# Ten of eleven gated sections with the weights loaded into TensorE and the tokens streamed, in a one-core decoder layer

## The chip, the core and the metric

The kernel runs on one NeuronCore of a Trainium2 chip. The metric is the device time of one execution in microseconds; the median of three runs is compared.

## The reference, cut to what matters

One decoder layer on 256 tokens of 2048 features: an attention mixer, a layer norm, a gated feed-forward unit with 5632 inner features, a second layer norm. The change lies in the gated unit:

```
def swiglu(x, w_gate, w_up, w_down):
    return (jax.nn.silu(x @ w_gate) * (x @ w_up)) @ w_down

x = layer_norm(ALPHA * x + h, ln1_g[i], ln1_b[i])
x = layer_norm(ALPHA * x + swiglu(x, ffn_w_gate[i], ffn_w_up[i], ffn_w_down[i]), ln2_g[i], ln2_b[i])
```

All data are float32. `x` is 256 x 2048, `w_gate` and `w_up` are 2048 x 5632, `w_down` is 5632 x 2048.

## The kernel before

Every product is made from three matmuls on parts that TensorE takes in one pass: an operand is split into a rounded part `hi` and a remainder `lo` (`split`, L67: ScalarE writes `hi`, VectorE writes `lo`), and hi·hi, hi·lo and lo·hi are accumulated in PSUM. Each matmul instruction comes with a weight load (LDWEIGHTS, shown as engine PEld) of its 128x128 stationary operand.

The weights pass through once as a stream of sections: four for query, key and value (`q`), two for the output projection (`o`), eleven for gate and up (`f0` to `f10`, `FU`), one for the down projection (`d`). A section `f_i` takes 512 columns of gate and 512 of up, over 2048 contraction rows: eight pairs of 128-row slices. The SyncE queue loads a piece (a pair, 512 columns), ScalarE and VectorE split it, and TensorE uses it. The order is written out by hand: `blocks` is a list of blocks of matmuls, each for one pair and one half `m` of the tokens (128 of them), alternating between the halves; pieces are loaded and split `AHEAD` = 3 blocks before their first use, and other work is hung behind numbered blocks with `after` and `before`. Engines work through their instructions in that order.

In `block` (L215) the 128 tokens of a half are the stationary operand (`lh`, `ll`) and 512 weight columns stream past them: per slice and half two matmuls of L227 and L228 for each of gate and up, then one of L231 for each. So the sums `acc` have tokens on partitions and gate or up columns along the free side; four banks of PSUM serve a section (two halves, gate and up). There are eight banks.

The down projection wants the gated values the other way round, with inner features on partitions. So `gate_evac` (L412) takes silu of the gate bank on ScalarE and multiplies it with the up bank on VectorE into `hn`, and two blocks later `gate_t` (L420) turns `hn` by four TensorE transposes of 128x128 into a bank `ht`, which ScalarE copies to `hT`. `split_h` splits it before the down projection uses it. The layer norm's output is turned the same way in `ln1_t` (L370) into `x1T`, features on partitions: one pair of tiles for each half `m` and 1024 features.

Other places that the text below speaks of: `at_o` (L298) is the last product of a head of attention; it has six matmuls at L309, three that stream 256 columns and three that stream 128, each with a load of its own. The down projection's blocks run through the same `block` as before; a pair there has 48 matmuls.

Of the kernel before, what the change touches and what calls it, by code (L numbers as in the profile page):

```python
# [10 lines left out]
F = mybir.dt.float32  # L11
R = mybir.dt.float32r
AF = mybir.ActivationFunctionType
OP = mybir.AluOpType

P = 128
S = 256
# [8 lines left out]
CW = 512  # L26
# [15 lines left out]
def decoder_layer(ctx: ExitStack, tc: tile.TileContext, x, xt, rel_bias, w_qkv, w_o, g1, b1, gb1,  # L42
                  w_gate, w_up, w_down, g2, b2, c_ident, c_hot, c_mask, out):
    nc = tc.nc
# [7 lines left out]
    def p4(shape, dt, name):  # L52
        return sb.tile(shape, dt, tag="p4", bufs=P4, name=name)

    def s2(shape, dt, name):
        return sb.tile(shape, dt, tag="s2", bufs=S2, name=name)
# [4 lines left out]
    def bank(name):  # L61
        return ps.tile([P, CW], F, tag="b", bufs=8, name=name)

    def f32(t):
        return t.bitcast(F)

    def split(hi, lo, src):  # L67
        nc.scalar.activation(hi, src, AF.Copy)  # L68
        nc.vector.tensor_tensor(lo, src, f32(hi), op=OP.subtract)  # L69
# [59 lines left out]
        hi, lo = xT[kt // 4]  # L129
        return hi[:, kt % 4, m * P:(m + 1) * P], lo[:, kt % 4, m * P:(m + 1) * P]  # L130

    # ---- sections of the weight stream
    oT = {}

    def o_lhs(kt, m):
# [3 lines left out]
    x1T = {}  # L139

    def x1_lhs(kt, m):
        hi, lo = x1T[m, kt // 8]
        return hi[:, kt % 8, :], lo[:, kt % 8, :]

    hS = {}

# [5 lines left out]
    WO = [Sec(f"o{i}", [(w_o, 2 * i + c) for c in range(2)], 8, o_lhs) for i in range(2)]  # L152
    NF = FF // CW
    FU = [Sec(f"f{i}", [(w_gate, i), (w_up, i)], 8, x1_lhs) for i in range(NF)]
    DN = Sec("d", [(w_down, c) for c in range(4)], FF // (2 * P), h_lhs)

    blocks, ticks = [], {}

    def add(sec, pairs, m, chunks=None, ks=(0, 1)):
        blocks.append((sec, pairs, m, range(len(sec.chunks)) if chunks is None else chunks, ks))  # L160
        return len(blocks) - 1

    def alternate(sec, a, b):
        for p in range(a, b):
            add(sec, [p], 0)
            add(sec, [p], 1)
# [8 lines left out]
    k = 8 - SKEW_WO  # L175
# [2 lines left out]
    f0_t = [[add(FU[0], [p], m) for p in range(SKEW_F)] for m in range(2)]  # L178
    alternate(FU[0], SKEW_F, 8)
    for s in FU[1:]:  # L180
        alternate(s, 0, 8)
    k = DN.npair - SKEW_D
    alternate(DN, 0, k)
    dn_p = list(range(k, DN.npair))
# [2 lines left out]
    first, last = {}, {}  # L187
# [4 lines left out]
    start = {k: t - AHEAD for k, t in first.items()}  # L192
# [13 lines left out]
    def split_piece(s, p, c):  # L206
# [5 lines left out]
        split(hi, lo, r)  # L212
        s.pieces[p, c] = (hi, lo)

    def block(s, pairs, m, chunks, ks):  # L215
        for c in chunks:
            if (m, c) not in s.acc:
                s.acc[m, c] = bank(f"acc_{s.name}_{m}_{c}")
        nk = 2 * s.npair
        for p in pairs:  # L220
            for k in ks:
                kt = 2 * p + k
                lh, ll = s.lhs(kt, m)
                for c in chunks:
                    hi, lo = s.pieces[p, c]
                    a = s.acc[m, c]
                    nc.tensor.matmul(a, lh, hi[:, k, :], start=kt == 0, stop=False)  # L227
                    nc.tensor.matmul(a, lh, lo[:, k, :], start=False, stop=False)  # L228
                for c in chunks:
                    hi, lo = s.pieces[p, c]  # L230
                    nc.tensor.matmul(s.acc[m, c], ll, hi[:, k, :], start=False, stop=kt == nk - 1)  # L231

    # ---- attention
    SC = HD ** -0.5
    grp = {}

# [85 lines left out]
            steps += one  # L322
        return steps

    # ---- layer norms
    y_t, ln = {}, {}

    def load_ln(gam, bet, name):
# [16 lines left out]
    def ych(m, c):  # L345
        return y_t[m, c // 2][:, (c % 2) * CW:(c % 2 + 1) * CW]
# [21 lines left out]
        nc.vector.tensor_scalar(y, y, ln["mv", m][:, 0:1], ln["r", m], op0=OP.subtract, op1=OP.mult)  # L368

    def ln1_t(m, c):  # L370
        if c % 2 == 0:
            x1T[m, c // 2] = (p4([P, 8, P], R, "x1h"), p4([P, 8, P], R, "x1l"))
        src = ych(m, c)
        b = bank("tr")
        t = s2([P, CW], F, "x1f")
        for j in range(4):
            js = slice(j * P, (j + 1) * P)
            nc.tensor.transpose(out=b[:, js], in_=src[:, js], identity=ident)
        for j in range(4):
            js = slice(j * P, (j + 1) * P)  # L380
            k = 4 * c + j
            g, s = gbT[:, k:k + 1], gbT[:, 16 + k:17 + k]
            if j < 3:
                nc.scalar.activation(t[:, js], b[:, js], AF.Identity, scale=g, bias=s)
            else:
                nc.vector.tensor_scalar(t[:, js], b[:, js], g, s, op0=OP.mult, op1=OP.add)
        hi, lo = x1T[m, c // 2]
        a = 4 * (c % 2)
        split(hi[:, a:a + 4, :], lo[:, a:a + 4, :], t.rearrange("p (j c) -> p j c", j=4))

    def ln1_affine(m, c):
        y = ych(m, c)
# [13 lines left out]
            eng.tensor_tensor(y, y, pch(1, c), op=OP.add)  # L406
        nc.sync.dma_start(out[m * P:(m + 1) * P, c * CW:(c + 1) * CW], y)

    # ---- gated unit
    hn, hT = {}, {}  # L410

    def gate_evac(i, m):  # L412
# [7 lines left out]
    def gate_t(i, m):  # L420
# [5 lines left out]
            nc.tensor.transpose(out=b[:, j * P:(j + 1) * P], in_=t[:, j * P:(j + 1) * P], identity=ident)  # L426
        nc.scalar.activation(hT[i][:, :, m * P:(m + 1) * P], b.rearrange("p (j c) -> p j c", j=4), AF.Copy)

    def split_h(i):
        t = hT.pop(i)  # L430
        hi, lo = p4([P, 4, S], R, f"hh{i}"), p4([P, 4, S], R, f"hl{i}")
        split(hi, lo, t)
        hS[i] = (hi, lo)

    # ---- what goes between the blocks
    pre, post = {}, {}

    def before(t, f, *a):
# [2 lines left out]
    def after(t, f, *a):  # L441
        post.setdefault(t, []).append((f, a))
# [25 lines left out]
    for m, at in ((0, [wo_t[1][0], wo_t[1][0], wo_t[1][1], f0_t[0][0]]),  # L468
                  (1, [f0_t[0][2], f0_t[0][2], f0_t[0][3], f0_t[1][0]])):
        for c in range(4):  # L470
            after(at[c], ln1_t, m, c)
    after(first["f1", 0], load_ln, g1, b1, "ln1")
    for m in range(2):
        for c in range(4):
            after(first["f1", 0] + 8 + 2 * (4 * m + c), ln1_affine, m, c)
    for i in range(NF):
        for m in range(2):
            t = last[f"f{i}", m]
            after(t, gate_evac, i, m)
            after(min(t + 2, first["d", 0]), gate_t, i, m)  # L480
    after(dn_t[0][0] - 12, load_ln, g2, b2, "ln2")
    for i in range(NF):
        t = first["d", 2 * i]
        before(t - 3 if i else t - 1, split_h, i)
# [13 lines left out]
    s = Q[0]  # L498
# [8 lines left out]
    for k in range(2):  # L507
        split_x(0, slice(k, k + 1))
        for c in range(3):
            hi, lo = s.pieces[0, c]  # L510
            split(hi[:, k, :], lo[:, k, :], s.raws[0, c][0][:, k, :])
    n = 0
    for t, blk in enumerate(blocks):
        for f, a in pre.get(t, []):
            f(*a)
        while n < len(order) and order[n][0] <= t:
            _, _, ss, p = order[n]
            if ss is Q[0]:
                load_x(p, slice(0, 2))
                split_x(p, slice(0, 2))  # L520
            for c in range(len(ss.chunks)):
                split_piece(ss, p, c)
            n += 1
        block(*blk)
        for f, a in post.get(t, []):
            f(*a)
# [49 lines left out]
```

## Time and profile before

| | us |
|---|---|
| median of three runs | 1147.78 (1147.64 to 1148.76) |
| span of the profiled execution, first to last instruction | 1145.1 |
| TensorE busy in it | 1125.9 (98%) |
| VectorE busy | 612.3 (53%) |
| ScalarE busy | 492.2 (43%) |

The profiled execution's own time beyond its span is not given apart; its span lies 2.7 us under the median. TensorE's two rows, PE and PEld, overlap: a weight load runs while an earlier matmul streams. Matmuls overlap as well, so the mean duration of one matmul is longer than the distance from its start to the next one's start. The distance of starts (called the pitch below) is what adds up to time.

### The profile page before, as it was taken

Reading aid. Unit: us, or ns where it says so; the run is one execution under the profiler, and the core shown is the slowest. Engines: PE = TensorE matmul, PEld = TensorE weight load, DVE = VectorE, ACT = ScalarE, POOL = GpSimd, SP = SyncE. Lnnn points to the kernel's source line nnn. Section 1 sums busy time; section 2 is a strip of 40 time slices with the busy share of each in tenths; the row PEclk is TensorE's granted clock in tenths of the full one; section 3 lists DMA queues with packets and bytes.
Section 4 is the critical chain, followed back from the end, with each engine's and each line's share of the span. In section 5 each row is a group of like instructions: output and inputs, shape, how many; then the busy total and the mean of one; then the engine's idle time right before and its main releaser. Section 6 shows DMA issues by size and latency. Waiting matters only on the chain.

```text
span 1145.1 us, 13392 instructions
## 1 busy us (share of the span) xinstructions
PE 1125.9 (98%) x5139; PEld 929.8 (81%) x5139; DVE 612.3 (53%) x737; ACT 492.2 (43%) x623; POOL 12.6 (1%) x20
## 2 busy tenths in 40 slices
PE   9989999999999999999999999999999999999995
PEld 6868888888888888888888888888888888888884
DVE  6535556664568664582452543542544555454456
ACT  6434444444455474362452442542533544344320
POOL 0000000000000000000000000000000000000002
PEclk9999999999999999999999999999999999999998
DMA  9996555554466627663653744745647565548611
GB/s 336 233 249 234 177 172 165 184 177 158 158 224 215 245 82 266 224 196 138 254 186 139 264 144 153 256 144 185 225 142 258 174 222 199 196 147 309 205 56 74
DMA packets 62816, 222.29 MB, mean 194 GB/s; under 512 B 7104, under 2 KB 7536, under 8 KB 62752
## 3 DMA queue, kind: packets, MB, share of 16 engines
q1 hardware_dynamic: 61472, 216.19, 54.3%
q0 software_dynamic: 1280, 5.24, 3.0%
q8 instruction: 40, 0.66, 0.2%
q14 instruction: 24, 0.20, 0.1%
HBM read 216.16 MB, written 5.24 MB: 193 GB/s over the span
## 4 chain that ended last, share of the span: by engine, by line
PE 93%; DMA 3%; issue 2%; DVE 1%; POOL 0%; ACT 0%; SPq 0%; DVEq 0%; POOLq 0%; ACTq 0%
PE acc_f L227 14%; PE acc_f L228 14%; PE acc_f L231 14%; PE acc_q L227 7%; PE acc_q L231 7%; PE acc_q L228 7%; PE acc_d L228 6%; PE acc_d L231 6%; PE acc_d L227 6%; DMA r_q<-in_w_qkv 3%; PE acc_o L227 3%; PE acc_o L228 3%; PE acc_o L231 3%; PE ov L309 1%; PE lg L266 1%
## 5 line engine op out<-in xcount | busy, mean ns | idle before, releaser
L227 PE MATMUL acc_f<-wh_f,x1h 128*128 128x512 f32 x704 | 276.4, 393 | 0.0
L228 PE MATMUL acc_f<-wl_f,x1h 128*128 128x512 f32 x704 | 274.2, 389 | 0.0
L69 DVE TENSOR_TENSOR wl_f<-r_f,wh_f 128x1024 fp32r<-128x1024 f32 x176 | 207.7, 1222 | 100.5 <-ACT wh_f L68 72.7
L231 PE MATMUL acc_f<-wh_f,x1l 128*128 128x512 f32 x704 | 216.9, 389 | 0.0
L68 ACT ACTIVATE wh_f<-r_f 128x1024 fp32r<-128x1024 f32 x176 | 177.2, 1054 | 78.9 <-PE acc_f L228 56.0
L69 DVE TENSOR_TENSOR wl_d<-r_d,wh_d 128x1024 fp32r<-128x1024 f32 x88 | 103.2, 1221 | 96.7 <-ACT wh_d L68 65.9
L231 PEld LDWEIGHTS acc_f<-wh_f,x1l 128*128 128x128 f32 x704 | 132.2, 188 | 27.8
L227 PEld LDWEIGHTS acc_f<-wh_f,x1h 128*128 128x128 f32 x704 | 132.2, 188 | 26.8
L228 PEld LDWEIGHTS acc_f<-wl_f,x1h 128*128 128x128 f32 x704 | 132.3, 188 | 26.7
L227 PE MATMUL acc_q<-wh_q,xh 128*128 128x512 f32 x372 | 149.2, 401 | 3.8 <-ACT qn L243 3.8
L228 PE MATMUL acc_q<-wl_q,xh 128*128 128x512 f32 x372 | 146.1, 393 | 1.0 <-DVE wl_q L69 1.0
L227 PE MATMUL acc_d<-wh_d,hh 128*128 128x512 f32 x352 | 137.0, 389 | 0.0
L228 PE MATMUL acc_d<-wl_d,hh 128*128 128x512 f32 x352 | 136.9, 389 | 0.0
L69 DVE TENSOR_TENSOR wl_q<-r_q,wh_q 128x1024 fp32r<-128x1024 f32 x93 | 109.5, 1222 | 50.2 <-ACT wh_q L68 49.6
L68 ACT ACTIVATE wh_d<-r_d 128x1024 fp32r<-128x1024 f32 x88 | 87.0, 1050 | 100.9 <-PE acc_d L228 79.7
L68 ACT ACTIVATE wh_q<-r_q 128x1024 fp32r<-128x1024 f32 x93 | 93.4, 1054 | 39.4 <-DMA r_q<-in_w_qkv 39.0
L231 PE MATMUL acc_q<-wh_q,xl 128*128 128x512 f32 x372 | 105.7, 392 | 0.0
L231 PE MATMUL acc_d<-wh_d,hl 128*128 128x512 f32 x352 | 99.9, 389 | 0.0
L417 DVE TENSOR_TENSOR hn<-acc_f,sg 128x512 f32<-128x512 f32 x22 | 15.1, 688 | 138.7 <-ACT sg L415 138.7
L227 PEld LDWEIGHTS acc_q<-wh_q,xh 128*128 128x128 f32 x372 | 70.3, 189 | 18.3 <-ACT qn L243 4.1
L228 PEld LDWEIGHTS acc_q<-wl_q,xh 128*128 128x128 f32 x372 | 70.4, 189 | 15.2 <-DVE wl_q L69 1.9
L231 PEld LDWEIGHTS acc_q<-wh_q,xl 128*128 128x128 f32 x372 | 70.3, 189 | 15.1
(102 smaller groups left out, 948.1 us busy)
## 6 DMA issues: line engine op xcount, KB each, us to landing
r_q<-in_w_qkv SPq DMA_DIRECT2D x93, 512.0 KB, 5.0
r_f<-in_w_gate SPq DMA_DIRECT2D x88, 512.0 KB, 4.6
r_f<-in_w_up SPq DMA_DIRECT2D x88, 512.0 KB, 5.0
r_d<-in_w_down SPq DMA_DIRECT2D x88, 512.0 KB, 4.6
r_o<-in_w_o SPq DMA_DIRECT2D x32, 512.0 KB, 4.4
rows<-rs POOLq DMA_DIRECT2D x1, 3072.0 KB, 35.9
bias<-rows POOLq DMA_DIRECT2D x4, 512.0 KB, 7.7
y<-in_x SPq DMA_DIRECT2D x4, 512.0 KB, 8.6
```

The lines of the kernel that those rows point to most:

```text
L68: nc.scalar.activation(hi, src, AF.Copy)
L69: nc.vector.tensor_tensor(lo, src, f32(hi), op=OP.subtract)
L227: nc.tensor.matmul(a, lh, hi[:, k, :], start=kt == 0, stop=False)
L228: nc.tensor.matmul(a, lh, lo[:, k, :], start=False, stop=False)
L231: nc.tensor.matmul(s.acc[m, c], ll, hi[:, k, :], start=False, stop=kt == nk - 1)
L266: nc.tensor.matmul(b[:, o:o + n], a[:, qs], c[:, ks], start=i == 0, stop=i == 2)
L309: nc.tensor.matmul(b[:, o:o + w], a[:, m, js], c[:, ks:ks + w], start=n == 0, stop=n == 5)
L417: nc.vector.tensor_tensor(t, s.acc[m, 1], sg, op=OP.mult)
```

## The change

Section `f0` stays as it was. In `f1` to `f10` a block is one slice `k` of a pair, for all 256 tokens, and `block_t` makes the 128 weight columns `js` of a piece the stationary operand and streams the 256 tokens of `x1T` past them. The sums then have inner features on partitions; a bank holds two of a piece's four column groups, side by side. `gate_direct` takes silu of the two gate banks and multiplies them with the two up banks straight into `hT`, behind the section's last block. `gate_evac` and `gate_t` stay for `f0` alone. `x1T` becomes one pair of tiles for each four slices with both halves of the tokens beside each other.

```diff
     for s in FU[1:]:
-        alternate(s, 0, 8)
+        for p in range(8):
+            for k in range(2):
+                add(s, [p], None, ks=[k])
...
+    def block_t(s, pairs, chunks, ks):
+        nk = 2 * s.npair
+        for c in chunks:
+            for h in range(2):
+                if (c, h) not in s.acc:
+                    s.acc[c, h] = bank(f"acc_{s.name}_{c}_{h}")
+        for p in pairs:
+            for k in ks:
+                kt = 2 * p + k
+                xh, xl = x1T[kt // 4]
+                xh, xl = xh[:, kt % 4, :], xl[:, kt % 4, :]
+                for c in chunks:
+                    hi, lo = s.pieces[p, c]
+                    for j in range(4):
+                        a = s.acc[c, j // 2][:, (j % 2) * S:(j % 2 + 1) * S]
+                        js = slice(j * P, (j + 1) * P)
+                        nc.tensor.matmul(a, hi[:, k, js], xh, start=kt == 0 and j % 2 == 0, stop=False)
+                        nc.tensor.matmul(a, hi[:, k, js], xl, start=False, stop=False)
+                        nc.tensor.matmul(a, lo[:, k, js], xh, start=False, stop=kt == nk - 1 and j % 2 == 1)
...
     def ln1_t(m, c):
-        if c % 2 == 0:
-            x1T[m, c // 2] = (p4([P, 8, P], R, "x1h"), p4([P, 8, P], R, "x1l"))
+        if m == 0:
+            x1T[c] = (p4([P, 4, S], R, "x1h"), p4([P, 4, S], R, "x1l"))
...
+    def gate_direct(i):
+        s = FU[i]
+        hT[i] = p4([P, 4, S], F, f"hT{i}")
+        for h in range(2):
+            sg = s2([P, CW], F, "sg")
+            nc.scalar.activation(sg, s.acc[0, h], AF.Silu)
+            nc.vector.tensor_tensor(hT[i][:, 2 * h:2 * h + 2, :], s.acc[1, h].rearrange("p (j c) -> p j c", j=2),
+                                    sg.rearrange("p (j c) -> p j c", j=2), op=OP.mult)
...
-    for i in range(NF):
-        for m in range(2):
-            t = last[f"f{i}", m]
-            after(t, gate_evac, i, m)
-            after(min(t + 2, first["d", 0]), gate_t, i, m)
+    for m in range(2):
+        after(last["f0", m], gate_evac, 0, m)
+        after(last["f0", m] + 2, gate_t, 0, m)
+    for i in range(1, NF):
+        after(last[f"f{i}", None], gate_direct, i)
```

TensorE's rows at the start of a section before: the second slice of the first block of `f4` and what follows it (names are out<-streamed operand, stationary operand; `acc_f4_1_0` is half 1, gate).

```order
L227 MATMUL acc_f4_0_0_4739<-wh_f4_0_0_4673,x1h_3366 128x512
L228 MATMUL acc_f4_0_0_4739<-wl_f4_0_0_4674,x1h_3366 128x512
L227 MATMUL acc_f4_0_1_4740<-wh_f4_0_1_4679,x1h_3366 128x512
L228 MATMUL acc_f4_0_1_4740<-wl_f4_0_1_4680,x1h_3366 128x512
L231 MATMUL acc_f4_0_0_4739<-wh_f4_0_0_4673,x1l_3367 128x512
L231 MATMUL acc_f4_0_1_4740<-wh_f4_0_1_4679,x1l_3367 128x512
L426 MATMUL ht_4754<-ident_76,hn_4709 128x128 x4
L227 MATMUL acc_f4_1_0_4772<-wh_f4_0_0_4673,x1h_3486 128x512
```

The same place of section `f5` in the changed kernel: the end of `f4` and the first matmuls of the first block (`acc_f5_0_1` is gate, the second bank).

```order
L233 MATMUL acc_f4_1_1_5289<-x1h_3452,wh_f4_7_1_5622 128x256
L234 MATMUL acc_f4_1_1_5289<-x1l_3453,wh_f4_7_1_5622 128x256
L235 MATMUL acc_f4_1_1_5289<-x1h_3452,wl_f4_7_1_5623 128x256
L233 MATMUL acc_f5_0_0_5777<-x1h_3366,wh_f5_0_0_5676 128x256
L234 MATMUL acc_f5_0_0_5777<-x1l_3367,wh_f5_0_0_5676 128x256
L235 MATMUL acc_f5_0_0_5777<-x1h_3366,wl_f5_0_0_5677 128x256
```

The operands changed places, each matmul streams 256 columns in place of 512, and the transposes of the section before are gone; a block now has 24 matmuls in place of 12.

## Rows read from the trace of the kernel before

**Rows 1.** The page: busy time of TensorE, and its granted clock in 40 slices

```profile
PE 1125.9 (98%) x5139; PEld 929.8 (81%) x5139; DVE 612.3 (53%) x737; ACT 492.2 (43%) x623; POOL 12.6 (1%) x20
...
PEclk9999999999999999999999999999999999999998
```

**Rows 2.** The page: the chain that ended last, by engine

```profile
PE 93%; DMA 3%; issue 2%; DVE 1%; POOL 0%; ACT 0%; SPq 0%; DVEq 0%; POOLq 0%; ACTq 0%
```

**Rows 3.** Groups of instructions: busy us, mean ns, idle before; sections f and transposes

```profile
L227 PE MATMUL acc_f<-wh_f,x1h 128*128 128x512 f32 x704 | 276.4, 393 | 0.0
L228 PE MATMUL acc_f<-wl_f,x1h 128*128 128x512 f32 x704 | 274.2, 389 | 0.0
L231 PE MATMUL acc_f<-wh_f,x1l 128*128 128x512 f32 x704 | 216.9, 389 | 0.0
...
L426 PE MATMUL ht<-ident,hn 128*128 128x128 f32 x88 | 13.0, 272 | 0.0
```

**Rows 4.** Timeline of PE around two turnings (start us, length, instruction)

```profile
494.24 0.62 PE L231 MATMUL acc_f<-wh_f,x1l 128*128 128x512 f32 x2
494.70 0.60 PE L426 MATMUL ht<-ident,hn 128*128 128x128 f32 x4
495.05 0.47 PE L227 MATMUL acc_f<-wh_f,x1h 128*128 128x512 f32 x1
495.36 0.39 PE L228 MATMUL acc_f<-wl_f,x1h 128*128 128x512 f32 x1
495.59 0.39 PE L227 MATMUL acc_f<-wh_f,x1h 128*128 128x512 f32 x1
495.82 0.40 PE L228 MATMUL acc_f<-wl_f,x1h 128*128 128x512 f32 x1
496.06 0.62 PE L231 MATMUL acc_f<-wh_f,x1l 128*128 128x512 f32 x2
...
539.18 0.60 PE L426 MATMUL ht<-ident,hn 128*128 128x128 f32 x4
```

**Rows 5.** Windows: one section, busy us of each engine (records), clock, DMA

```profile
494.49:538.97 44.48, 44.48 (x202) 36.83 (x201) 24.30 (x25) 18.28 (x20) 0.00 (x0) 1.00 0.54 189
```

**Rows 6.** The chain in order of time: two pieces of the down projection

```profile
903.34 0.91 PE acc_d L231 x4
...
1099.17 0.91 PE acc_d L231 x4
```

**Rows 7.** Timeline of PE: the matmuls of one at_o, 256 and 128 columns

```profile
349.67 0.28 PE L309 MATMUL ov<-pth,vh 128*128 128x256 f32 x1
349.78 0.28 PE L309 MATMUL ov<-ptl,vh 128*128 128x256 f32 x1
349.90 0.28 PE L309 MATMUL ov<-pth,vl 128*128 128x256 f32 x1
350.02 0.22 PE L309 MATMUL ov<-pth,vh 128*128 128x128 f32 x1
350.08 0.28 PE L309 MATMUL ov<-ptl,vh 128*128 128x128 f32 x1
350.19 0.27 PE L309 MATMUL ov<-pth,vl 128*128 128x128 f32 x1
```

**Rows 8.** Timeline of PEld: two weight loads there

```profile
350.02 0.19 PEld L309 LDWEIGHTS ov<-ptl,vh 128*128 128x128 f32 x1
350.13 0.19 PEld L309 LDWEIGHTS ov<-pth,vl 128*128 128x128 f32 x1
```

**Rows 9.** Timelines of PE, ACT and DVE where f10 ends and d begins

```profile
892.29 0.39 PE L227 MATMUL acc_d<-wh_d,hh 128*128 128x512 f32 x1
...
894.78 0.58 ACT L415 ACTIVATE sg<-acc_f 128x512 f32<-128x512 f32 x1
...
892.27 4.62 DVE L69 TENSOR_TENSOR wl_d<-r_d,wh_d 128x1024 fp32r<-128x1024 f32 x4
896.81 0.68 DVE L417 TENSOR_TENSOR hn<-acc_f,sg 128x512 f32<-128x512 f32 x1
```

More of the change, by code (lines that the diff above doesn't have):

```diff
@@ L141, in x1_lhs @@
     def x1_lhs(kt, m):
-        hi, lo = x1T[m, kt // 8]
-        return hi[:, kt % 8, :], lo[:, kt % 8, :]
+        hi, lo = x1T[kt // 4]
+        return hi[:, kt % 4, m * P:(m + 1) * P], lo[:, kt % 4, m * P:(m + 1) * P]
     hS = {}
@@ L213, in split_piece @@
         s.pieces[p, c] = (hi, lo)
+    def block_t(s, pairs, chunks, ks):
[17 more added lines that the diff above has]
+                        nc.tensor.matmul(a, lo[:, k, js], xh, start=False, stop=kt == nk - 1 and j % 2 == 1)
     def block(s, pairs, m, chunks, ks):
+        if m is None:
+            return block_t(s, pairs, chunks, ks)
         for c in chunks:
@@ L386, in ln1_t @@
                 nc.vector.tensor_scalar(t[:, js], b[:, js], g, s, op0=OP.mult, op1=OP.add)
-        hi, lo = x1T[m, c // 2]
-        a = 4 * (c % 2)
-        split(hi[:, a:a + 4, :], lo[:, a:a + 4, :], t.rearrange("p (j c) -> p j c", j=4))
+        hi, lo = x1T[c]
+        ms = slice(m * P, (m + 1) * P)
+        split(hi[:, :, ms], lo[:, :, ms], t.rearrange("p (j c) -> p j c", j=4))
     def ln1_affine(m, c):
```

## The prediction

> **What bounds the kernel now.** I read the page first. TensorE is busy for 98% of the span and its granted clock stands in the top tenth in all slices but the last [rows 1]; the chain that ended last is TensorE for 93% [rows 2]. The groups of instructions then say that inside the gated unit TensorE never waits: 3 x 704 matmuls of 512 columns with 0.0 us idle before them, and the same for the 88 transposes [rows 3]. So this stage is limited by how fast TensorE takes matmul after matmul, and a change in it is worth what it changes in the sum of pitches. A mean duration (389 ns) is of no use for that, since matmuls overlap; the distance of starts is.
>
> The timeline gives the period of a section: the transposes of one section start at 494.70 and of the next at 539.18 [rows 4], so a section takes 44.48 us. A window of that length has TensorE busy throughout, a clock of 1.00, VectorE at 24.30 us and ScalarE at 18.28 us, and DMA at 0.54 [rows 5]. Nothing but TensorE is near its limit.
>
> **What a section is made of.** It has 192 matmuls of 512 columns (16 slices, 2 halves, 2 weights, 3 products) and 8 transposes. The pitch at 512 columns comes from the down projection, whose matmuls have the same shape: from 903.34 to 1099.17 [rows 6] there are 72 half-slices of 12 matmuls (2.72 us each in the chain), 864 in all, so 195.83 / 864 = 0.2267 us. 192 x 0.2267 = 43.52 us. A turning: the two matmuls ahead of it start at 494.24, the next matmul at 495.05 [rows 4]; 0.81 less two pitches (0.45) leaves 0.36 for four transposes, 0.72 for a section's two turnings. Together 44.24. The last 0.24 is what the matmuls right behind a turning lose: from 495.05 to 495.36 it is 0.31, then 0.23, 0.23 and 0.24 [rows 4].
>
> **What the change removes.** The transposes of `f1` to `f10`, ten times 0.72 + 0.24 = 9.6 us of TensorE's time, on the path. (Those of `f10` lay in the first block of the down projection; they count the same.) It also removes 20 copies of `ht` from ScalarE; these were hidden, ScalarE being busy for 18 us of 44, and are worth nothing.
>
> **What it adds.** The columns streamed stay the same: 192 x 512 = 384 x 256. The number of matmuls, and of weight loads, doubles to 384 a section. So all hangs on one price, the pitch of a matmul of 256 columns with its own weight load, in a long row. With the section at 44.48 us, the change breaks even where that pitch is 44.48 / 384 = 0.1158 us.
>
> The trace has such matmuls only three in a row, in attention. Starts are at 349.67, 349.78, 349.90 and 350.02 [rows 7]: pitches of 0.11, 0.12 and 0.12. The first follows matmuls of 512 columns, the later ones follow their own kind. Two lines can be drawn through this. If the pitch goes with the columns alone, 256 cost half of 0.2267, that is 0.1133, and that is the first of the three. If each matmul has a fixed part beside its columns, the columns at the full clock cost 512 / 2.4 GHz = 0.2133 us, the fixed part is 0.0134, and 256 columns cost 0.1067 + 0.0134 = 0.120, and that is the second and third. The weight load sets a floor that lies lower: where 128 columns stream, two loads stand 350.13 - 350.02 = 0.11 apart [rows 8], and one matmul follows another by 0.06 where its load had begun ahead, by 0.11 where not [rows 7]. A row of 256-column matmuls thus is only just not limited by its loads. I take 0.120, because in a row of 384 each matmul follows its own kind, and the pitches that do so are 0.12.
>
> Bounds: from below 0.1133 (half of the 512 pitch; the loads' 0.11 forbids much less). From above I put on 0.120 what 512-column matmuls lose for a while after short ones: 495.36 to 496.06 is three pitches of 0.233 [rows 4], 0.007 over the steady 0.2267, so 0.127.
>
> A rule that speaks for the lower bound: the Trainium skill, "TensorE: Matmul & The Clock Gate", section "Back-to-back issue gap", gives the warm gap as the columns divided by 2.4 GHz plus about 2.5 ns. By that rule 256 columns would cost 0.109 us, a section 41.9 us, and the change would save some 25 us. It gives 0.216 us for 512 columns; this trace shows 0.2267 for matmuls with their loads, so the trace does not agree.
>
> **The sum.** A section: 384 x 0.120 = 46.08 us against 44.48, so +1.60; ten sections +16.0 us (+25.6 for matmuls, -9.6 for turnings). The rest is hidden:
>
> - Silu and product are as many and as large as before (two each a section); they are only bunched behind the section's last block. The next section uses the other four banks, so TensorE doesn't wait for them; they have a section's length.
> - The one place where the cover is thin is the start of the down projection, which needs all eight banks. Its first half begins where `f10` ends, at 892.29 in the trace before; its second half begins 24 pitches (5.4 us) later, at 897.7. Four splits of weights stand ahead of the gated product on VectorE, which began at 896.81 after splits from 892.27 on, and silu at 894.78 [rows 9]. Two silus then end near 896.0 and free the first two banks in time. The two products of 0.68 end near 897.5 and 898.2; the up banks they free are wanted by the fifth and the seventh matmul of the second half, at 898.6 and 899.1. If the splits are late by 1 us, TensorE waits some 0.5 us once. I count nothing.
> - Loads and splits keep their block numbers (16 blocks a section before and now), so SyncE's queue and the split order stay; a block gets some 0.04 us longer. The other layout of `x1T` changes no count.
>
> The sum is made against the span of 1145.1; the median lies 2.7 us above it, which I carry over unchanged: 1147.8 + 16.0 = **1163.8 us**.
>
> **The rivals.**
>
> 1. *The fixed part is no part of it; the pitch goes with the columns.* Then 384 x 0.1133 = 43.51 us a section, -0.97, ten times -9.7: 1138.1 us, faster. The mechanism is that the extra loads ride wholly beside the streaming, and the turnings are won. For it: the first pitch of the three is 0.11, and loads can stand 0.11 apart. Against it: the two that follow are 0.12. It decides from a pitch under 0.1158. Chance 13%. (The rule of the Trainium skill, "TensorE: Matmul & The Clock Gate", "Back-to-back issue gap", would put the pitch there.)
> 2. *In between.* The mean of the three, (350.02 - 349.67) / 3 = 0.1167, or up to 0.119, if the first kind of pitch returns now and then: 44.8 to 45.7 us, +3 to +12, around 1155 us. Chance 14%.
> 3. *The long row is slower than the short one.* Three matmuls can live on a lead that the 512-column ones ahead of them left; 384 can't, and with a load and a matmul every 0.12 us in place of every 0.23 the loads may lag. At the upper bound 384 x 0.127 = 48.8 us, +4.3, ten times +43: 1191 us; half of it gives 1177. For it: matmuls do lose some time behind short ones [rows 4]; against it: the transposes, whose loads come as often, follow one another without idle time [rows 3]. Chance 15%.
> 4. *Nothing measurable:* the loss by the fixed part and the gain by the turnings cancel, at a pitch within 0.1152 and 0.1164. Chance 3%.
>
> **How the numbers follow.** My forecast, a pitch of 0.119 to 0.122, gets the other 55%: 1160 to 1171 us, with 1163.8 for 0.120. The range of 1149 to 1183 us reaches down through rival 2 (pitch 0.1163) and up into rival 3 (pitch 0.125); it leaves out rivals 1 and 4 and the far part of rival 3, some 2 in 10. Within 0.2% (2.3 us) of 1147.8 is what a measurement of this kernel can't tell from no change. Faster takes rival 1 (0.13), same rival 4 (0.03), slower the rest (0.84).
>
> **What would show it.** In the profile after: 20 x 4 transposes fewer, eight left; 3840 matmuls of 256 columns in place of 1920 of 512; a section of 46.1 us between the first matmuls of two sections, with pitches of 0.12 in the timeline, TensorE without idle time and the clock at 1.00. ScalarE and VectorE should be idle for longer. It would be wrong if the pitch inside a section is 0.113 (rival 1) or 0.125 and more (rival 3), if a section begins with a wait for a bank, if the splits fall behind (a wait for `wl_f`), or if the second half of the down projection begins with a wait for VectorE of more than a microsecond.

## The result, and the profile after

The changed kernel takes 1164.66 us (median of four, 1163.5 to 1165.61) beside 1147.71 for the kernel before: a ratio of 1.0143, 95% interval 1.013 to 1.0157: slower, by 1.4%. The forecast was 1163.8 us, slower.

The page of the changed kernel, busy time and granted clock, then its chain by engine:

```profile
PE 1142.8 (98%) x6979; PEld 1023.2 (88%) x6979; DVE 614.9 (53%) x737; ACT 486.6 (42%) x603; POOL 12.6 (1%) x20
...
PEclk9989999999999999999999999999999999999998
...
PE 91%; DMA 5%; issue 2%; DVE 1%; ACT 0%; SPq 0%; POOL 0%; DVEq 0%; ACTq 0%; POOLq 0%
```

The reader is to see that nothing about the limits changed: TensorE at 98% and at its full clock in the gated unit, the other engines where they were [rows 1, 2]. TensorE has 6979 matmuls in place of 5139: 1920 more, 80 fewer.

Its groups of instructions (busy us, mean ns, idle before) hold the whole change:

```profile
L233 PE MATMUL acc_f<-x1h,wh_f 128*128 128x256 f32 x1280 | 362.4, 283 | 0.0
L235 PE MATMUL acc_f<-x1h,wl_f 128*128 128x256 f32 x1280 | 362.2, 283 | 0.0
L234 PE MATMUL acc_f<-x1l,wh_f 128*128 128x256 f32 x1280 | 362.2, 283 | 0.0
...
L450 PE MATMUL ht<-ident,hn 128*128 128x128 f32 x8 | 1.2, 272 | 0.0
```

Twice as many matmuls of half the width as in [rows 3], still without idle time, and eight transposes in place of 88. The pitch, from TensorE's timeline (start us, length) inside a section:

```profile
699.81 0.28 PE L234 MATMUL acc_f<-x1l,wh_f 128*128 128x256 f32 x1
699.93 0.28 PE L235 MATMUL acc_f<-x1h,wl_f 128*128 128x256 f32 x1
700.05 0.28 PE L233 MATMUL acc_f<-x1h,wh_f 128*128 128x256 f32 x1
...
701.97 0.28 PE L234 MATMUL acc_f<-x1l,wh_f 128*128 128x256 f32 x1
```

From the first to the last of these are 18 pitches: 2.16 / 18 = 0.120 us, the same at every step. It is the second and third pitch of [rows 7], not the first. The section, from ScalarE's timeline, where the pair of silus comes once a section:

```profile
632.57 1.32 ACT L458 ACTIVATE sg<-acc_f 128x512 f32<-128x512 f32 x2 [14.18 <-PE acc_f L235]
...
678.65 1.32 ACT L458 ACTIVATE sg<-acc_f 128x512 f32<-128x512 f32 x2 [14.06 <-PE acc_f L235]
```

46.08 us a section, where it was 44.48 [rows 4, 5]. The thin place, the start of the down projection, from the timelines of VectorE and of TensorE:

```profile
901.80 1.22 DVE L69 TENSOR_TENSOR wl_d<-r_d,wh_d 128x1024 fp32r<-128x1024 f32 x1
...
909.71 1.23 DVE L69 TENSOR_TENSOR wl_d<-r_d,wh_d 128x1024 fp32r<-128x1024 f32 x1 [3.10 <-ACT sg L458]
910.85 1.28 DVE L459 TENSOR_TENSOR hT<-acc_f,sg 128x512 f32<-128x512 f32 x2
...
911.01 0.40 PE L251 MATMUL acc_d<-wh_d,hh 128*128 128x512 f32 x1
...
916.48 0.39 PE L251 MATMUL acc_d<-wh_d,hh 128*128 128x512 f32 x1
```

The last two products end at 912.1, 4.3 us before the second half begins, and there is no wait. The four splits that ran in the kernel before from the start of the down projection on, ahead of the product [rows 9], are over earlier here: they run from 901.80 to 910.94, while TensorE is still at `f10`. In the kernel before, the work of the first half of the tokens stood ahead of them, and ScalarE waited 7.78 us for that half's sums:

```profile
889.54 0.60 ACT L415 ACTIVATE sg<-acc_f 128x512 f32<-128x512 f32 x1 [7.78 <-PE acc_f L231]
890.04 1.05 ACT L68 ACTIVATE hh<-hT 128x1024 fp32r<-128x1024 f32 x1
890.99 3.90 ACT L68 ACTIVATE wh_d<-r_d 128x1024 fp32r<-128x1024 f32 x4
```

In the changed kernel the silus of `f10` stand behind the section's last block and start at 909.05 on ScalarE, when three of the four splits are done.

### The profile page after: what moved, and what is told of

The parts are those of the page before. It is cut to its first block, busy times and chain, and to the rows that moved or that the text cites. A ratio compares the mean times of both kernels' runs of the same rounds, so it can differ in the third digit from the quotient of the medians.

```text
span 1163.2 us, 17056 instructions
## 1 busy us (share of the span) xinstructions
PE 1142.8 (98%) x6979; PEld 1023.2 (88%) x6979; DVE 614.9 (53%) x737; ACT 486.6 (42%) x603; POOL 12.6 (1%) x20
## 4 chain that ended last, share of the span: by engine, by line
PE 91%; DMA 5%; issue 2%; DVE 1%; ACT 0%; SPq 0%; POOL 0%; DVEq 0%; ACTq 0%; POOLq 0%
PE acc_f L235 13%; PE acc_f L234 13%; PE acc_f L233 13%; PE acc_d L255 6%; PE acc_d L252 6%; PE acc_d L251 6%; PE acc_q L251 6%; PE acc_q L255 6%; PE acc_q L252 6%; DMA r_q<-in_w_qkv 5%; PE acc_o L251 3%; PE acc_o L252 3%; PE acc_o L255 3%; PE acc_f L251 1%; PE acc_f L252 1%
## 5 line engine op out<-in xcount | busy, mean ns | idle before, releaser
L233 PE MATMUL acc_f<-x1h,wh_f 128*128 128x256 f32 x1280 | 362.4, 283 | 0.0
L235 PE MATMUL acc_f<-x1h,wl_f 128*128 128x256 f32 x1280 | 362.2, 283 | 0.0
L234 PE MATMUL acc_f<-x1l,wh_f 128*128 128x256 f32 x1280 | 362.2, 283 | 0.0
L68 ACT ACTIVATE wh_f<-r_f 128x1024 fp32r<-128x1024 f32 x176 | 181.1, 1057 | 157.9 <-PE acc_f L234 69.2
L234 PEld LDWEIGHTS acc_f<-x1l,wh_f 128*128 128x128 f32 x1280 | 245.8, 192 | 0.0
L233 PEld LDWEIGHTS acc_f<-x1h,wh_f 128*128 128x128 f32 x1280 | 245.8, 192 | 0.0
L235 PEld LDWEIGHTS acc_f<-x1h,wl_f 128*128 128x128 f32 x1280 | 245.7, 192 | 0.0
L252 PEld LDWEIGHTS acc_q<-wl_q,xh 128*128 128x128 f32 x372 | 70.5, 190 | 14.9 <-DVE wl_q L69 1.6
L252 PEld LDWEIGHTS acc_d<-wl_d,hh 128*128 128x128 f32 x352 | 66.1, 188 | 13.7
```

The lines of the kernel that those rows point to most:

```text
L233: nc.tensor.matmul(a, hi[:, k, js], xh, start=kt == 0 and j % 2 == 0, stop=False)
L234: nc.tensor.matmul(a, hi[:, k, js], xl, start=False, stop=False)
L235: nc.tensor.matmul(a, lo[:, k, js], xh, start=False, stop=kt == nk - 1 and j % 2 == 1)
```

## The experiments

All times are medians beside the kernel before on the same chip (1147.8 to 1147.9 us), with the ratio and its 95% interval.

**The turnings alone.** The kernel before without the transposes of `f1` to `f10`:

```diff
...
-        for j in range(4):
-            nc.tensor.transpose(out=b[:, j * P:(j + 1) * P], in_=t[:, j * P:(j + 1) * P], identity=ident)
-        nc.scalar.activation(hT[i][:, :, m * P:(m + 1) * P], b.rearrange("p (j c) -> p j c", j=4), AF.Copy)
+        if i == 0:
+            for j in range(4):
+                nc.tensor.transpose(out=b[:, j * P:(j + 1) * P], in_=t[:, j * P:(j + 1) * P], identity=ident)
+        src = b if i == 0 else t
+        nc.scalar.activation(hT[i][:, :, m * P:(m + 1) * P], src.rearrange("p (j c) -> p j c", j=4), AF.Copy)
```

> The kernel before, with the gated values of f1 to f10 left unturned (the transposes are left out, ScalarE copies the unturned tile, so the values are in the wrong places; the copies themselves stay). Theory: a section's two turnings are on TensorE's path and worth 0.72 us for the transposes and 0.24 us for the matmuls behind them, ten sections 9.6 us: 1138.1 us, the section 43.5 us. Rival, that the turnings ride beside other work and the change removed nothing: 1147.7 us.

Measured: 1138.14 us, 0.9914 (0.9899 to 0.9928). ScalarE's timeline, first silu of two sections:

```profile
577.08 0.60 ACT L415 ACTIVATE sg<-acc_f 128x512 f32<-128x512 f32 x1 [18.20 <-PE acc_f L231]
...
620.60 0.60 ACT L415 ACTIVATE sg<-acc_f 128x512 f32<-128x512 f32 x1 [17.71 <-PE acc_f L231]
```

43.52 us a section. The gain of the change is real, and is the 9.6 us that were reckoned: 1147.77 - 1138.14 = 9.63.

**The number of matmuls alone.** The kernel before, tokens loaded as before, turnings kept, each matmul of `f1` to `f10` cut in two:

```diff
...
+        parts = [slice(0, S), slice(S, CW)] if cut else [slice(0, CW)]
...
-                    nc.tensor.matmul(a, lh, hi[:, k, :], start=kt == 0, stop=False)
+                    for n, q in enumerate(parts):
+                        nc.tensor.matmul(a[:, q], lh, hi[:, k, q], start=kt == 0 and n == 0, stop=False)
...
```

> The kernel before with tokens in TensorE and turnings as they were, but each matmul of 512 columns in f1 to f10 cut into two of 256 columns, each with its own load. Theory, a fixed part of 0.0133 us for each matmul with its load, whichever operand is loaded: 384 x 0.120 + 0.96 = 47.04 us a section, ten times +2.56: 1173.3 us. Rival, that it is the swap of operands (freshly split weights loaded, tokens streamed) that costs, not the number: pitch 0.1133, 43.5 + 0.96 us a section, 1147.7 us.

Measured: 1173.07 us, 1.0219 (1.0204 to 1.0235). TensorE's timeline; a row with x2 holds two matmuls:

```profile
700.19 0.40 PE L230 MATMUL acc_f<-wh_f,x1h 128*128 128x256 f32 x2
700.43 0.40 PE L232 MATMUL acc_f<-wl_f,x1h 128*128 128x256 f32 x2
700.67 0.40 PE L230 MATMUL acc_f<-wh_f,x1h 128*128 128x256 f32 x2
```

0.24 for two, 0.120 for one. Which operand is loaded does not matter; the number does. The two runs together, -9.6 and +25.3 us, give +15.7 beside the +16.95 of the whole change.

**The order of the products.** The changed kernel with no two matmuls in a row on the same region of PSUM:

```diff
-                    for j in range(4):
+                    for n, (w, v) in enumerate(((hi, xh), (hi, xl), (lo, xh))):
+                        for j in range(4):
...
```

> The changed kernel with the three products of a piece taken in turn over the four column groups, so that no two matmuls in a row add to the same region of PSUM. Theory: no change, pitch 0.120, 1164.7 us. Rival, that adding three times in a row to the same 256 columns costs the extra 0.0067 us: pitch 0.1133, a section 43.5 us, 1139 us.

Measured: 1163.99 us, 1.0142 (1.0125 to 1.0159): no difference from the changed kernel. Adding to the same columns costs nothing.

**Fewer, wider matmuls in the changed kernel.** `x1T` holds hi and lo beside each other, and the weights' hi streams both at once:

```diff
-                        nc.tensor.matmul(a, hi[:, k, js], xh, start=kt == 0 and j % 2 == 0, stop=False)
-                        nc.tensor.matmul(a, hi[:, k, js], xl, start=False, stop=False)
+                        nc.tensor.matmul(a, hi[:, k, js], xx, start=kt == 0 and j % 2 == 0, stop=False)
...
```

> The changed kernel with hi of the weights streaming the tokens' hi and lo parts as one matmul of 512 columns; lo of the weights streams hi in 256 as before. (The two column groups of a bank are added up on top of each other, so the sums are not the reference's; the columns streamed are as many.) 128 + 128 matmuls a section in place of 384. Theory, a fixed part for each matmul: 128 x (0.2267 + 0.120) = 44.38 us a section, 1.7 less than 46.08, ten times -17: 1147.7 us. Rival, that loading weights and streaming tokens is slow by itself: 1164.7 us.

Measured: 1155.81 us, 1.0067 (1.0052 to 1.0082). Both theories missed: about half of the 17 us came back (1164.66 - 1155.81 = 8.85). TensorE's timeline:

```profile
700.13 0.40 PE L233 MATMUL acc_f<-x,wh_f 128*128 128x512 f32 x1
700.36 0.28 PE L234 MATMUL acc_f<-x,wl_f 128*128 128x256 f32 x1
700.48 0.40 PE L233 MATMUL acc_f<-x,wh_f 128*128 128x512 f32 x1
700.72 0.28 PE L234 MATMUL acc_f<-x,wl_f 128*128 128x256 f32 x1
...
702.96 0.40 PE L233 MATMUL acc_f<-x,wh_f 128*128 128x512 f32 x1
```

700.13 to 702.96 holds eight pairs: 0.354 us a pair, not 0.2267 + 0.120 = 0.347. 512 columns behind 256 take 0.23 to 0.24. So rows of one width add up by the fixed part, and alternating widths cost 0.007 more a pair. The sections are 45.23 us apart (584.79 to 630.02 on ScalarE).

**The same matmuls, widths grouped.** Four of 512, then four of 256; the edit is against the run before this one:

```diff
                         nc.tensor.matmul(a, hi[:, k, js], xx, start=kt == 0 and j % 2 == 0, stop=False)
+                    for j in range(4):
+                        a = s.acc[c, j // 2]
+                        js = slice(j * P, (j + 1) * P)
```

> The kernel of the wide run with its order changed: for a piece and slice first the four matmuls of 512 columns, then the four of 256 (sums as wrong as there). There a 512-column matmul took 0.2365 us behind one of 256, in place of 0.2267. If that loss comes with each change of width: a quarter of the changes, 128 x (0.2267 + 0.120) + 32 x 0.0067 = 44.6 us a section, 1150 us. If a 512-column matmul stays slower for several matmuls behind a short one, as behind a turning: about 0.2333 for all of them, 45.2 us a section, 1155.8 us as there.

Measured: 1151.53 us, 1.0032 (1.0021 to 1.0042), between the two. The timeline, groups of four, and the second matmul of the first group by itself:

```profile
699.80 1.09 PE L233 MATMUL acc_f<-x,wh_f 128*128 128x512 f32 x4
700.73 0.64 PE L237 MATMUL acc_f<-x,wl_f 128*128 128x256 f32 x4
701.21 1.09 PE L233 MATMUL acc_f<-x,wh_f 128*128 128x512 f32 x4
702.14 0.63 PE L237 MATMUL acc_f<-x,wl_f 128*128 128x256 f32 x4
702.61 0.63 PE L233 MATMUL acc_f<-x,wh_f 128*128 128x512 f32 x2
```

```profile
700.03 0.40 PE L233 MATMUL acc_f<-x,wh_f 128*128 128x512 f32 x1
```

Four of 512 take 0.93, 0.2325 each, where four of their own kind take 0.907; four of 256 take 0.48 and 0.47, 0.119 each. The loss does not lie in the first of a group alone: the other three, from 700.03 to 700.73, take 0.70 where three of their own kind take 0.68. So wide matmuls stay slow for several behind narrow ones, as behind a turning [rows 4], at nearly the 0.2333 of the second theory; a loss at each change alone is not borne out. The narrow ones are a little faster than either theory had them, and the section comes to 44.91 us (581.88 to 626.79 on ScalarE). What makes the wide ones slow stays open.

**The price by width.** The kernel before, the matmuls of each section cut to a width of its own:

```diff
+WIDTHS = {"f1": (480, 1), "f2": (448, 1), "f3": (384, 1), "f4": (320, 1), "f5": (288, 1),
+          "f6": (224, 2), "f7": (192, 2), "f8": (160, 3), "f9": (128, 4), "f10": (256, 2)}
...
+        width, n_parts = WIDTHS.get(s.name, (CW, 1))
+        parts = [slice(i * width, (i + 1) * width) for i in range(n_parts)]
...
```

> The kernel before with the matmuls of f1 to f10 narrowed to 480, 448, 384, 320, 288, twice 224, twice 192, three times 160, four times 128 and twice 256 columns (columns beyond are left out after the first slice, so the values are not the reference's): one look, for the pitch at each width. A fixed part of 0.0133 us beside the columns at 2.4 GHz: 0.213, 0.200, 0.173, 0.147, 0.133 and 0.120 at 480, 448, 384, 320, 288 and 256. Rival, a price in proportion to the columns (0.443 ns each) over a floor of 0.120 that the loads set: 0.2125, 0.198, 0.170, 0.142, 0.1275 and 0.120. At 224 and below the first gives 0.107 and less, unless the loads stop it at 0.11 to 0.12.

Measured: 1161.57 us, a single run that mixes the widths, so its time decides nothing. TensorE's timeline in the sections with 480, 448, 384, 320, 288, 224 and 128 columns:

```profile
480.41 0.38 PE L232 MATMUL acc_f<-wh_f,x1h 128*128 128x480 f32 x1
...
481.06 0.38 PE L234 MATMUL acc_f<-wl_f,x1h 128*128 128x480 f32 x1
...
520.21 0.37 PE L232 MATMUL acc_f<-wh_f,x1h 128*128 128x448 f32 x1
...
521.04 0.37 PE L238 MATMUL acc_f<-wh_f,x1l 128*128 128x448 f32 x1
...
550.22 0.33 PE L232 MATMUL acc_f<-wh_f,x1h 128*128 128x384 f32 x1
...
550.92 0.33 PE L238 MATMUL acc_f<-wh_f,x1l 128*128 128x384 f32 x1
...
580.23 0.31 PE L232 MATMUL acc_f<-wh_f,x1h 128*128 128x320 f32 x1
...
580.82 0.46 PE L238 MATMUL acc_f<-wh_f,x1l 128*128 128x320 f32 x2
...
609.90 0.29 PE L232 MATMUL acc_f<-wh_f,x1h 128*128 128x288 f32 x1
...
610.43 0.42 PE L238 MATMUL acc_f<-wh_f,x1l 128*128 128x288 f32 x2
...
640.06 0.39 PE L232 MATMUL acc_f<-wh_f,x1h 128*128 128x224 f32 x2
...
640.51 0.39 PE L232 MATMUL acc_f<-wh_f,x1h 128*128 128x224 f32 x2
...
790.00 0.61 PE L232 MATMUL acc_f<-wh_f,x1h 128*128 128x128 f32 x4
790.44 0.61 PE L234 MATMUL acc_f<-wl_f,x1h 128*128 128x128 f32 x4
```

The first pair of rows is three pitches apart, each other pair four: 0.217 at 480, 0.2075 at 448, 0.175 at 384, 0.1475 at 320, 0.1325 at 288, 0.1125 at 224 and 0.11 at 128. Starts are given to 0.01, so four pitches give one to about 0.0025. The fixed part fits 384, 320 and 288 (0.173, 0.147, 0.133); a price in proportion to columns is refuted there (0.170, 0.142, 0.1275). At 448 the pitch lies above both lines by 0.007 or more, at 480 by 0.003 or 0.004, which nothing here explains. From 256 columns to 512, each among its own kind, the pitch grows by 0.2267 - 0.120 = 0.1067, which is 256 columns at 2.4 GHz; the rest is what each matmul pays whatever its width. From 224 down the pitch hardly falls. That fits the floor of 0.11 that the loads were reckoned to set [rows 7, 8], and a matmul of 256 columns at 0.120 lies just above it.

**Both kernels in bfloat16.** The split parts, hi and lo, in bfloat16, with the same three products, on the kernel before and on the changed one:

```diff
-R = mybir.dt.float32r
+R = mybir.dt.bfloat16
...
-        nc.vector.tensor_tensor(lo, src, f32(hi), op=OP.subtract)
+        nc.vector.tensor_tensor(lo, src, hi, op=OP.subtract)
```

> The kernel before with both parts of every split operand in bfloat16 in place of rounded float32 (three products as before, less exact). If the fixed part of 0.0133 us belongs to the instruction: no change of pitch, 1147.7 us. If it belongs to loads or operands of four bytes, it shrinks: at most 4704 matmuls x 0.0133 = 62 us less, 1085 us.

> The changed kernel with both parts in bfloat16. If the fixed part belongs to the instruction: 1164.7 us. If it belongs to four-byte loads or operands, it shrinks and twice the number of matmuls costs less: at most (3840 + 2784) x 0.0133 = 88 us less, 1076 us, and then the change is faster than the same kernel without it, by up to the turnings' 9.6 us.

Measured: 1090.88 us (1090.38 to 1091.59), 0.9501 (0.9487 to 0.9515), for the order before; 1087.49 us (1086.6 to 1087.7), 0.9469 (0.9455 to 0.9483), for the changed one. Both are faster than either kernel in float32, by 57 of the 62 us and 77 of the 88 us that were given as the most, and the sign of the change turns: it now wins 3.4 us. TensorE's timeline of the order before, then of the changed one:

```profile
699.82 0.38 PE L225 MATMUL acc_f<-wl_f,x1h 128*128 128x512 bf16 x1
...
701.76 0.59 PE L228 MATMUL acc_f<-wh_f,x1l 128*128 128x512 bf16 x2
```

```profile
699.80 0.27 PE L232 MATMUL acc_f<-x1h,wl_f 128*128 128x256 bf16 x1
...
700.78 0.27 PE L232 MATMUL acc_f<-x1h,wl_f 128*128 128x256 bf16 x1
```

Nine pitches in 1.94, 0.2156 at 512; nine in 0.98, 0.109 at 256. Less the columns at 2.4 GHz (0.2133, 0.1067) a fixed part of 0.0023 is left, in place of 0.0134. Twice the matmuls cost 192 x 0.0023 = 0.4 us a section, and the turnings are won. The sections agree: they are 42.31 us apart (590.78 to 633.09 on ScalarE) and 41.92 us (591.71 to 633.63), against 192 x 0.2156 = 41.4, so 0.9 for turnings is won and 0.5 for matmuls paid, 3.9 us in ten sections. That both operands and loads got shorter at once leaves open which of them carried the fixed part; the weight loads are recorded with 98 ns in place of 188 to 192 (groups of instructions).

The rule that was cited against the forecast, in the Trainium skill, "TensorE: Matmul & The Clock Gate", "Back-to-back issue gap" (columns at 2.4 GHz plus about 2.5 ns), is what these two bfloat16 runs show, loads included. For float32 parts the traces differ from it: 13 ns. The same section of the Trainium skill calls that formula the gap of an isolated matmul, which the prediction left out. For a stream of weight loads and matmuls the Trainium skill gives there about 131 ns at 512 columns. No run here agrees with that: the shortest steady pitch at 512 is 215.6 ns.

## Why the prediction was right, point by point

- *What bounds the kernel.* Right: the sum of pitches set the time of the gated unit in every float32 run; its matmuls had no idle time before them in the changed kernel either.
- *What is removed.* Right in size, shown by the run without transposes: 9.6 us reckoned, 9.63 measured.
- *What is added.* Right: 384 x 0.120 = 46.08 us, to the last digit. The choice that carried the forecast was to take the second and third pitch of [rows 7], those that follow their own kind, and not the first. That it came out so exactly is in part luck. The starts in [rows 7] are given to 0.01, so the two pitches, 0.24 together, bound one to 0.115 to 0.125 only, and the break-even of 0.1158 lies inside; what set 0.120 was the fixed part, worked out at 512 columns and taken to hold at 256. The reading beneath it, a fixed part for each matmul with its load, is shown by the cut matmuls (+25.3 us for the doubled number, +25.6 reckoned) and by the widths; it holds for rows of one width from 256 to 384 and at 512. It does not hold for mixed widths (0.354 a pair, 0.347 reckoned) nor at 448 and 480.
- *The thin place.* Counting nothing was right, but the picture behind it was not. The prediction had four splits between the start of the down projection and the gated product, which left the up banks 1.1 and 0.9 us before they are wanted, by the fifth and seventh matmul of the second half. In the changed kernel these splits are over before the down projection begins, and the banks are free at 912.1, some 5 us before the fifth matmul (916.48 + 4 x 0.2267 = 917.4).
- *The total.* +16.0 reckoned, +16.95 between the medians, with an interval of 14.9 to 18.0 (0.013 and 0.0157 of 1147.71). The profiled spans differ by 18.1. By the timelines 1.9 of that is there before the gated unit begins (its first matmul starts at 401.45 before and at 403.33 after), where both kernels have the same matmuls; in the profiles of the other float32 runs that start lies between 401.8 and 404.2, in no order by kernel, so this part reads as scatter. The first matmul of the down projection starts at 892.29 and 911.01, so the gated unit itself has grown by 18.7 - 1.9 = 16.8. Less the 0.96 for the eight transposes of `f10`, which the down projection no longer holds, that is 15.9 beside the 16.0 of the sum.
- *The rivals.* The price by columns alone (13%) is refuted by the widths, the slower long row (15%) by the steady 0.120. That it lands between was refuted by the same rows, and that nothing is measurable by the interval, which begins at 14.9 us.

## What to carry to other kernels

Swapping the two operands of a matmul keeps the columns but can change the number of matmuls, and on an engine that never waits, as here, the fixed part of each is paid in full: 1920 more at 0.0133 us came to 25.6 us against 9.6 us of transposes saved. Read the pitch of the new shape from a row where it follows its own kind, in the element type at hand, before reckoning: with bfloat16 parts, which are less exact, the fixed part was 0.0023 and the same swap won 3.4 us. A mean duration would have told none of this (0.283 us beside a pitch of 0.120).

## What the hardware showed that was not expected

- A float32 matmul of 512 columns takes 0.23 to 0.24 us in a stream where matmuls of 256 or transposes stand between, and 0.2267 among its own kind.
- At 448 columns the float32 pitch is 0.2075, more than the 0.200 that the fixed part gives, while 384 takes 0.175 at most.
- PEld is busy for 88% of the span in the changed kernel, by loads that are recorded with 192 ns each (groups of instructions) but follow each other by 0.120 and, at 128 columns, by 0.11; so that share says little of how near the loads are to being the limit.
